# Two-layer hybrid decoder trunk: the MLP's up projection written in the down projection's form, with up and down units in one ordered stream

## The chip, the cores and the metric

The kernel runs on one core of one Trainium2 chip. The core has five engines with queues of their own: TensorE (PE) multiplies matrices and turns tiles, VectorE (DVE) and ScalarE (ACT) do elementwise work, GpSimd (POOL) does a little of it, and SyncE (SP) issues the DMAs. The metric is the device time of one execution in microseconds; lower is better. The kernel before takes 2218.81 us (median of three runs, 2218.77 to 2218.85).

## The reference

There are two layers over 256 tokens of width 2048, all in float32. A layer has a token-mixing part (gated linear attention beside stick-breaking attention, between one input and one output projection) and an MLP with 8192 hidden columns. The change is in the MLP:

```python
    mixed = jnp.concatenate([o_gla, o_sb], axis=-1)
    x = x + jnp.einsum('bse,ed->bsd', mixed, w_o)

    hm = rms_norm(x, mlp_norm)
    up = jnp.square(jax.nn.relu(jnp.einsum('bsd,df->bsf', hm, w_up)))
    return x + jnp.einsum('bsf,fd->bsd', up, w_down)
```

`w_up` is 2048 x 8192 and `w_down` 8192 x 2048, so each holds 64 MB per layer, and each layer multiplies 256 rows by both.

## The kernel before, in words

**Precision.** TensorE is fed with float32r, and each float32 operand is cut into a high part (a copy to float32r by ACT, L359 and L991) and a low part (the difference, by DVE, L361 and L992). A product of two operands is three matmuls: high by high, high by low, low by high.

**Residual and operands.** The residual stream lies in four tiles `xb[0..3]` of 128 partitions x 2 token blocks x 512 columns. `norm_operand` (L287) turns a tile on PE with the identity, four 128x128 turns to a bank, and writes the high and low parts of the turned, gain-scaled columns into operand tiles, a "pair" of two 128-row blocks each. The row factor of the norm isn't in the operand; it is applied later to the product.

**Up projection.** `mlp_up(q, g)` (L924) makes two times 256 hidden columns of quarter q. `unit_t` (L412) keeps the weights stationary and streams the activations: for each of the 16 row blocks and each of two 128-column halves one matmul of 512 columns (weight high by activations high and low side by side, L425) and one of 256 (weight low by activations high, L429). The result comes out with hidden columns on the partitions, which is what the down projection needs. `join` (L436) adds the two halves; then come the ReLU with the norm's row factor (L931, `row` laid along the free axis by `row_of`, L330), the square (L935), and `up_forms` (L942), which cuts the result into high and low (L939, L940). The scheduler orders this stage.

**Down projection.** `mlp_down(q)` (L962) adds quarter q's 2048 hidden rows into x in two units of 1024 output columns (`n2`). A unit runs over eight pairs j of row blocks. The activation block is now stationary and the weights stream, 512 columns to a matmul. An ordinary pair needs eight block products (two row blocks, two token blocks, two column halves) and has two steps of 12 matmuls. The pairs in `fast` (j = 1, 3, 5) use seven products of sums of blocks (a Winograd form of Strassen's scheme): `first` (L1038) makes three sums of the weights on DVE, `up_forms` has made three 128x128 sums of the activations before, and the pair has four steps of 6, 3, 6 and 6 matmuls. A unit so has 22 steps (0 to 21) and 5 x 24 + 3 x 21 = 183 matmuls, into eight PSUM banks m1 to m8. `drain` (after step 17), `drain_left` (after 20) and `drain_right` (after 21) add the banks into `xb`, one copy on ACT and 8 + 2 + 2 adds on DVE.

**Order.** PE, DVE and ACT take the down stage in an order written out by hand. Each step is prepared (sums, then `parts`: the high part on ACT, the low part on DVE) and appended to a queue; when four are in it (`LEAD`, L1099), the oldest one's matmuls are issued. So step k's matmuls stand behind the preparation of step k + 3, and what follows step k (a drain) stands on DVE and ACT in front of the preparation of step k + 4. The high and low tiles are a ring of four (L989, L990): step k + 4 is prepared into the tiles of step k, once its matmuls are through. Weights come in 1 MB loads on SP's queue, four pairs ahead. Each engine takes its instructions in this order, so one that waits holds back all behind it.

Of the kernel before, what the change touches and what calls it, by code (L numbers as in the profile page):

```python
# [16 lines left out]
P = 128  # L17
# [22 lines left out]
def trunk_kernel(  # L40
# [60 lines left out]
    ATT = ("v4", "lr", "lrT", "ha", "hh", "hl", "hA", "on", "dec", "S", "kdz")  # L101
    MLP = ("sx", "ts", "t4", "raw2")
# [9 lines left out]
    def down_psum():  # L112
        open_scope("psum", m=1)

# [155 lines left out]
    class Operand:  # L270


        def __init__(self):
            self.t = {}

# [11 lines left out]
    def norm_operand(op, n, key, l):  # L287

        for h2 in range(2):
            d = op.pair(2 * n + h2)  # L290
            pt = ps_tile()
            for j in range(2):
                for tt in range(NT):
                    c = (2 * h2 + j) * P
                    nc.tensor.transpose(  # L295
                        pt[:, j * T + tt * P : j * T + (tt + 1) * P],
                        xb[n][:, tt, c : c + P], ident,
                    )
            for j in range(2):
# [305 lines left out]
    for l in range(DEPTH):  # L605
# [296 lines left out]
        def residual(op, n, key, ll, ssq, acc, done):  # L902
            nc.vector.tensor_tensor(xb[n], acc, xb[n], ALU.add)
            after(1, lambda: norm_operand(op, n, key, ll))
            after(2, lambda: norm_squares(n, ssq))
            if n == 3:
                after(2, done)

# [3 lines left out]
        def mlp_stats():  # L912
            r = norm_finish(ssq)
            after(1, lambda: nxt.update(row=row_of(r)))

        for n in range(4):
            uo = unit(mixed, w_o[l], 0, n * 512, 512, (2, 3, 0, 1))
            residual(hm, n, "mlp", l, ssq, uo, mlp_stats)


        open_scope("sbuf", mlp=1)
        up = {}

        def mlp_up(q, g):  # L924
            if g == 0:
                up[q] = Operand()
                up[q].x = {}
            for b in range(2):
                i = 2 * g + b
# [8 lines left out]
        def split(d, t):  # L938
            nc.scalar.activation(d[:, :, 0, :], t, AF.Copy)  # L939
            nc.vector.tensor_tensor(d[:, :, 1, :], t, f32(d[:, :, 0, :]), ALU.subtract)  # L940

        def up_forms(op, i, t):  # L942


            if fast(i):
                a11, a21, a12, a22 = (t[:, k, r * P : (r + 1) * P] for k in range(2) for r in range(2))
                e = tmp("t2", [P, 3, P], bufs=4)
                d = op.x[i] = tmp("sx", [P, 3, 2, P], F32R, bufs=3)
                nc.vector.tensor_tensor(e[:, 2, :], a21, a11, ALU.subtract)
                nc.vector.tensor_tensor(a21, a21, a22, ALU.subtract)  # L950
                nc.vector.tensor_tensor(e[:, 0, :], a11, a21, ALU.subtract)
                nc.vector.tensor_tensor(e[:, 1, :], a12, e[:, 0, :], ALU.subtract)
                split(d, e)
            split(op.pair(i), t)

        def fast(i):
            return i in (1, 3, 5)

        hT = Operand()
        ssq2 = new_ssq()  # L960

        def mlp_down(q):  # L962


            op = up[q]
            end = q == 3 and l + 1 == DEPTH
            pairs = [(n2, j) for n2 in range(2) for j in range(8)]
            raws, banks = {}, {}
            begun = set()

            def load(x):
                if x >= len(pairs):
                    return
                n2, j = pairs[x]
                if x % 5 < 2:
                    r = tmp("raw2", [P, 2, 1024], bufs=2)
                else:
                    r = wpool.tile([P, 2, 1024], F32, tag="raw", name=nm("raw"))
                raws[x] = r
                r0 = (q * KT + 2 * j) * P  # L980
                nc.sync.dma_start(
                    r,
                    w_down[l][r0 : r0 + 2 * P, n2 * 1024 : (n2 + 1) * 1024].rearrange(
                        "(k p) n -> p k n", p=P
                    ),
                )

            def parts(r, n=2):
                hi = ppool.tile([P, 2, 512], F32R, tag="whi", name=nm("whi"), bufs=4)  # L989
                lo = ppool.tile([P, 2, 512], F32R, tag="wlo", name=nm("wlo"), bufs=4)  # L990
                nc.scalar.activation(hi[:, :n], r, AF.Copy)  # L991
                nc.vector.tensor_tensor(lo[:, :n], r, f32(hi[:, :n]), ALU.subtract)  # L992
                return hi, lo

            def mm(m, a, w, c, last):

                (ah, al), (wh, wl) = a, w
                o = banks[m]
                nc.tensor.matmul(o, ah, wh[:, c], start=m not in begun, stop=False)
                begun.add(m)  # L1000
                nc.tensor.matmul(o, ah, wl[:, c], start=False, stop=False)
                nc.tensor.matmul(o, al, wh[:, c], start=False, stop=last)

            def add(dst, a, b, sub=False):
                nc.vector.tensor_tensor(dst, a, b, ALU.subtract if sub else ALU.add)  # L1005

            def new_banks():
                begun.clear()
                for m in (5, 1, 6, 7, 2, 4, 3, 8):
                    banks[m] = pools["m"].tile([P, 512], F32, tag=f"m{m}", name=nm(f"m{m}_"))  # L1010

            def steps(x):

                n2, j = pairs[x]
                last = j == 7
                r = raws[x]
                d = op.t[j]
                x11, x21, x12, x22 = (xb[2 * n2 + c][:, tt, :] for c in range(2) for tt in range(2))

                def blk(k, tt):  # L1020
                    sl = slice(tt * P, (tt + 1) * P)
                    return d[:, k, 0, sl], d[:, k, 1, sl]

                def ext(i):
                    return op.x[j][:, i, 0, :], op.x[j][:, i, 1, :]

                def store(c, tt):
                    if end:
                        n = 2 * n2 + c
                        nc.sync.dma_start(  # L1030
                            ov[:, tt, n * 512 : (n + 1) * 512], xb[n][:, tt, :]
                        )

                if fast(j):
                    sums = {}
                    lastf = j == 5

                    def first():  # L1038
                        t13 = sums["t13"] = tmp("ts", [P, 2, 512], bufs=2)
                        t4 = sums["t4"] = tmp("t4", [P, 512], bufs=1)  # L1040
                        b12 = r[:, 0, 512:]
                        ends = r.rearrange("p k (c n) -> p (k c) n", c=2)[:, ::3, :]
                        nc.vector.tensor_tensor(  # L1043
                            t13, ends, b12.unsqueeze(1).to_broadcast([P, 2, 512]), ALU.add
                        )
                        add(b12, t13[:, 0, :], r[:, 1, 512:])
                        add(t4, b12, r[:, 1, :512])
                        return parts(r[:, 1, :].rearrange("p (c n) -> p c n", c=2))

                    def drain():  # L1050
                        dw = tmp("t2", [P, 512], bufs=4)
                        nc.scalar.activation(dw, banks[1], AF.Copy)
                        add(x12, banks[5], x12)
                        add(x22, banks[5], x22)
                        add(x11, banks[1], x11)
                        add(dw, banks[6], dw, True)
                        add(x12, dw, x12)
                        add(dw, banks[7], dw)
                        add(x21, x21, dw, True)
                        add(x22, dw, x22)  # L1060

                    return (
# [113 lines left out]
```

## Time and profile before

| what | time or share |
|---|---|
| median of three runs | 2218.81 us |
| the profiled execution, whole | 2219.26 us |
| its span (first to last instruction) | 2217.5 us |
| PE busy in it | 2208.2 us |
| DVE busy in it | 1627.6 us |
| ACT busy in it | 1170.7 us |
| DVE, wait for high parts by ACT at L359 | 417.7 us in 381 waits |
| ACT, wait for PE to free a high tile of the up stage (L425) | 338.1 us in 250 waits |

Busy times count each matmul with a modelled end that overlaps the next one, so PE's cost per instruction is read from the distance between starts, and not from the durations. Times in the rows of a timeline are microseconds from the start of the span. In a row, `x3` counts merged instructions, the first number is the start and the second the length, and what stands in square brackets is idle time of that engine ahead of it and what ended it. PEclk is the clock granted to TensorE, with 1.00 for full speed.

### The profile page before, as it was taken

How to read it: one execution, taken by the hardware profiler on the slowest of the kernel's cores; microseconds unless marked ns; L12 is line 12 of the kernel's file. 1: busy time of each engine (PE TensorE's matmuls, PEld its weight loads, DVE VectorE, ACT ScalarE, POOL GpSimd, SP SyncE). 2: the span in 40 equal slices, each digit the busy share in tenths (PEclk: the TensorE clock that was granted, in tenths of full speed). 3: DMA queues.
4: the chain of work that ended last, by engine and by line, in shares of the span. 5: the costliest groups of instructions: out<-in, count | busy, mean ns of one | idle time of the engine just before them, and what ended most of it. 6: DMA issues, size and time to landing. Idle time of an engine off the chain costs nothing.

```text
span 2217.5 us, 28469 instructions
## 1 busy us (share of the span) xinstructions
PE 2208.2 (100%) x11292; PEld 1857.2 (84%) x11292; DVE 1627.6 (73%) x2024; ACT 1170.7 (53%) x1499; POOL 39.1 (2%) x68
## 2 busy tenths in 40 slices
PE   9999999999999999999999999999999999999999
PEld 7988778888888888888888887788888888888887
DVE  5777556568868868967967775656697688688688
ACT  5555355555555455455556553545555555554553
POOL 0020000000000000000000200000000000000000
PEclk9999999999999999999999999999999999999999
DMA  6645446665664665665446544465656656656654
GB/s 225 196 153 168 139 149 229 189 190 190 209 189 172 222 184 179 206 198 188 172 136 197 171 158 142 150 233 184 190 183 216 190 189 208 185 177 217 186 178 141
DMA packets 250858, 409.05 MB, mean 184 GB/s; under 512 B 6651, under 2 KB 162883, under 8 KB 250725
## 3 DMA queue, kind: packets, MB, share of 16 engines
q1 hardware_dynamic: 250724, 407.24, 56.3%
q8 instruction: 88, 1.44, 0.3%
q14 instruction: 46, 0.37, 0.0%
HBM read 405.12 MB, written 2.10 MB: 184 GB/s over the span
## 4 chain that ended last, share of the span: by engine, by line
PE 98%; DVE 1%; issue 0%; DMA 0%; ACT 0%; POOL 0%; SPq 0%; POOLq 0%
PE acc L425 24%; PE acc L429 12%; PE acc L378 9%; PE acc L379 9%; PE acc L380 9%; PE ps L295 1%; PE ps L848 1%; PE ps L860 1%; PE ps L807 0%; PE ps L541 0%; PE ps L487 0%; DVE wlo L361 0%; PE ps L576 0%; PE ps L505 0%; DMA raw<-in_w_in_dram 0%
## 5 line engine op out<-in xcount | busy, mean ns | idle before, releaser
L361 DVE TENSOR_TENSOR wlo<-raw,whi 128x1024 fp32r<-128x1024 f32 (+2 forms) x530 | 630.3, 1193 | 418.7 <-ACT whi L359 417.7
L359 ACT ACTIVATE whi<-raw 128x1024 fp32r<-128x1024 f32 (+2 forms) x530 | 545.1, 1032 | 642.2 <-PE acc L425 338.1
L425 PE MATMUL acc<-act,whi 128*128 128x512 f32 x2304 | 813.2, 398 | 0.0
L429 PE MATMUL acc<-act,wlo 128*128 128x256 f32 x2304 | 645.1, 280 | 0.0
L425 PEld LDWEIGHTS acc<-act,whi 128*128 128x128 f32 x2304 | 432.9, 188 | 105.1
L429 PEld LDWEIGHTS acc<-act,wlo 128*128 128x128 f32 x2304 | 434.7, 189 | 0.4
L378 PE MATMUL acc<-whi,act 128*128 128x512 f32 (+2 forms) x960 | 368.1, 383 | 1.2 <-ACT act L303 0.9
L379 PE MATMUL acc<-wlo,act 128*128 128x512 f32 (+2 forms) x960 | 362.0, 377 | 0.4 <-DVE wlo L361 0.4
L380 PE MATMUL acc<-whi,act 128*128 128x512 f32 (+2 forms) x960 | 361.7, 377 | 0.0
L992 DVE TENSOR_TENSOR wlo<-raw,whi 128x1024 fp32r<-128x1024 f32 x256 | 305.6, 1221 | 48.2 <-ACT whi L991 44.6
L991 ACT ACTIVATE whi<-raw 128x1024 fp32r<-128x1024 f32 x256 | 266.4, 1059 | 122.9 <-PE acc L425 28.7
L378 PEld LDWEIGHTS acc<-whi,act 128*128 128x128 f32 x960 | 180.7, 188 | 36.5 <-issue 4.1
L380 PEld LDWEIGHTS acc<-whi,act 128*128 128x128 f32 x960 | 180.5, 188 | 33.9 <-issue 0.7
L379 PEld LDWEIGHTS acc<-wlo,act 128*128 128x128 f32 x960 | 180.7, 188 | 32.0 <-DVE wlo L361 1.2
L991 ACT ACTIVATE whi<-t 128x512 fp32r<-128x512 f32 x48 | 30.4, 633 | 157.1 <-DVE t L1005 45.1
L992 DVE TENSOR_TENSOR wlo<-ts,whi 128x1024 fp32r<-128x1024 f32 x48 | 58.8, 1225 | 2.3 <-ACT whi L991 2.3
L1043 DVE TENSOR_TENSOR ts<-raw 128x1024 f32<-128x1024 f32 x48 | 58.4, 1217 | 0.0
L940 DVE TENSOR_TENSOR act<-t,act 128x512 fp32r<-128x512 f32 x64 | 44.1, 689 | 10.9 <-ACT act L939 10.9
L991 ACT ACTIVATE whi<-ts 128x1024 fp32r<-128x1024 f32 x48 | 50.2, 1046 | 0.0
L440 DVE TENSOR_TENSOR t<-acc,t 128x512 f32<-128x512 f32 x72 | 49.2, 683 | 0.0
L935 ACT ACTIVATE t<-t 128x512 f32<-128x512 f32 x64 | 39.5, 617 | 12.8 <-DVE t L931 12.8
L931 DVE SCALAR_TENSOR_TENSOR t<-t,row 128x512 f32<-128x512 f32 x64 | 44.3, 692 | 2.2
(1160 smaller groups left out, 2760.0 us busy)
## 6 DMA issues: line engine op xcount, KB each, us to landing
raw<-in_w_down_dram SPq DMA_DIRECT2D x128, 1024.0 KB, 5.3
raw<-in_w_up_dram SPq DMA_DIRECT2D x128, 1024.0 KB, 5.8
raw<-in_w_in_dram SPq DMA_DIRECT2D x84, 1024.0 KB, 5.1
raw<-in_w_o_dram SPq DMA_DIRECT2D x32, 1024.0 KB, 5.0
raw<-in_w_in_dram SPq DMA_DIRECT2D x14, 512.0 KB, 6.6
raw<-in_w_in_dram SPq DMA_DIRECT2D x8, 544.0 KB, 3.8
out_dram<-xb SPq DMA_DIRECT2D x8, 256.0 KB, 2.2
xb<-in_x_dram SPq DMA_DIRECT2D x3, 512.0 KB, 7.6
```

Source lines behind the costliest of these rows:

```text
L359: newest["hi"] = nc.scalar.activation(h, r, AF.Copy).ins
L361: newest["lo"] = nc.vector.tensor_tensor(lo[:, q : q + step, :width], r, f32(h), ALU.subtract).ins
L378: nc.tensor.matmul(o, xh[:, sl], whi[:, j, :width], start=first, stop=False)
L379: nc.tensor.matmul(o, xh[:, sl], wlo[:, j, :width], start=False, stop=False)
L380: st["mm"] = nc.tensor.matmul(o, xl[:, sl], whi[:, j, :width], start=False, stop=last).ins
L425: nc.tensor.matmul(acc[:, f, :], whi[:, j, sl], op.both(k), start=(k == 0), stop=False, skip_group_check=True,)
L429: nc.tensor.matmul(acc[:, f, T:], wlo[:, j, sl], xh, start=False, stop=(k == KT - 1), skip_group_check=True,)
L440: nc.vector.tensor_tensor(t, acc[:, :, :T], t, ALU.add)
L931: nc.vector.scalar_tensor_tensor(t, t, 0.0, nxt["row"].unsqueeze(1).to_broadcast([P, 2, T]), ALU.max, ALU.mult,)
L991: nc.scalar.activation(hi[:, :n], r, AF.Copy)
L992: nc.vector.tensor_tensor(lo[:, :n], r, f32(hi[:, :n]), ALU.subtract)
L1043: nc.vector.tensor_tensor(t13, ends, b12.unsqueeze(1).to_broadcast([P, 2, 512]), ALU.add)
```

## The change

The up projection leaves `unit_t` and takes the form of the down projection: activation pairs of `hm` stationary, weights streaming, 1024 hidden columns to a unit, the same eight pairs with three of them by seven products, the same banks. `norm_operand` makes the sums of the activations for the three pairs (`sums=True`, `forms`). An up unit ends with tokens on the partitions, so its result has to be turned: `up_tail` combines the banks into two float32 tiles (one ACT copy and 4 + 2 + 2 adds on DVE) and applies the ReLU with the row factor on ACT, `turn` turns a tile on PE (eight 128x128 turns into two banks) and squares it out of PSUM on ACT, and `operand` cuts the pairs into high and low. For each up unit u this is done inside unit u + 1: `turn` stands behind steps 0 and 1 of it, `operand` behind steps 3, 4, 9 and 10.

All 16 units of a layer (two up and two down for each quarter) are now steps of one ordered stream with one queue; no stage is left to the scheduler, and the switch of PSUM pools between up and down is gone. The last part of the output projection's residual (n = 3), its `norm_operand` and the norm's statistics move into the first up unit. Gone are `mlp_up`, `join` for the up stage, `row_of` for the MLP, and the drains of the up stage.

In the order of the changed program, the instructions behind step 0 to step 10 of a unit that follows an up unit are, on ACT: high 3, two squares (turn 0), high 4, two squares (turn 1), high 5, high 6, cut of operand 0, high 7, two cuts of operand 1, high 8 to 12, cut of operand 2, high 13, cuts of operand 3, high 14. On DVE they are: the last two adds of the up unit, sums of pair 1 and low 2, low 3 to 6, cut of operand 0, low 7, four 128x128 sums and two cuts of operand 1, the sums of pair 3 and low 8, and so on.

```diff
@@ norm_operand @@
+    def fast(i):
+        return i in (1, 3, 5)
+
+    def split(d, t):
+        nc.scalar.activation(d[:, :, 0, :], t, AF.Copy)
+        nc.vector.tensor_tensor(d[:, :, 1, :], t, f32(d[:, :, 0, :]), ALU.subtract)
+
+    def forms(op, i, t, tag):
...
+            nc.vector.tensor_tensor(e[:, 2, :], a21, a11, ALU.subtract)
+            nc.vector.tensor_tensor(a21, a21, a22, ALU.subtract)
+            nc.vector.tensor_tensor(e[:, 0, :], a11, a21, ALU.subtract)
+            nc.vector.tensor_tensor(e[:, 1, :], a12, e[:, 0, :], ALU.subtract)
+            split(d, e)
+        split(op.pair(i), t)
+
-    def norm_operand(op, n, key, l):
+    def norm_operand(op, n, key, l, sums=False, banks=None):
...
+            if sums and fast(2 * n + h2):
...
+                forms(op, 2 * n + h2, t, "sxh")
+                continue
@@ the MLP @@
-        def mlp_up(q, g):
...
-                t = join(unit_t(hm, w_up[l], q * 2048 + i * 256))
-                nc.vector.scalar_tensor_tensor(
-                    t, t, 0.0, nxt["row"].unsqueeze(1).to_broadcast([P, 2, T]),
-                    ALU.max, ALU.mult,
-                )
-                nc.scalar.activation(t, t, AF.Square)
-                up_forms(up[q], i, t)
...
+        units = [(q, down, n2) for q in range(4) for down in range(2) for n2 in range(2)]
...
+        def up_tail(u):
...
+            def relu(h):
+                for tt in range(NT):
+                    nc.scalar.activation(
+                        y[h][:, tt, :], y[h][:, tt, :], AF.Relu, scale=rs["r"][:, tt : tt + 1]
+                    )
+
+            def sums():
...
+                nc.scalar.activation(y11, banks[1], AF.Copy)
+                add(dw, banks[6], y11, True)
+                add(y12, banks[5], dw)
+                add(y21, banks[7], dw)
+                add(y22, banks[5], y21)
+
+            def left():
+                add(y[0][:, 0, :], banks[2], y[0][:, 0, :])
+                add(y[0][:, 1, :], banks[4], y[0][:, 1, :], True)
+                relu(0)
+
+            def right():
+                add(y[1][:, 0, :], banks[3], y[1][:, 0, :])
+                add(y[1][:, 1, :], banks[8], y[1][:, 1, :])
+                relu(1)
...
+        def turn(u, h):
...
+            for i in range(2):
+                pt = bank(((5, 7), (1, 6))[h][i])
+                for j in range(2):
+                    for tt in range(NT):
+                        c = (2 * i + j) * P
+                        nc.tensor.transpose(
+                            pt[:, j * T + tt * P : j * T + (tt + 1) * P],
+                            y[h][:, tt, c : c + P], ident,
+                        )
+                nc.scalar.activation(t[:, i].rearrange("p j t -> p (j t)"), pt, AF.Square)
+
+        def operand(u, i):
...
+            forms(op, 4 * n2 + i, ys[u]["t", i // 2][:, i % 2], "sx")
...
+        def begin(u):
+
+            if u == 0:
+                def stats():
+                    norm_squares(3, ssq)
+                    rs["r"] = norm_finish(ssq)
+
+                return {
+                    0: lambda: norm_operand(hm, 3, "mlp", l, sums=True, banks=(5, 7)),
+                    4: stats,
+                }
+            if units[u - 1][1]:
+                return {}
+            p = u - 1
+            return {
+                0: lambda: turn(p, 0), 1: lambda: turn(p, 1),
+                3: lambda: operand(p, 0), 4: lambda: operand(p, 1),
+                9: lambda: operand(p, 2), 10: lambda: operand(p, 3),
+            }
...
+        def emit():
+            u, k, products, w = queue.pop(0)
...
+            products(w)
+            (sums, left, right), extra = tails[u]
+            if k in extra:
+                extra[k]()
+
+            for at, fn in ((17, sums), (20, left), (21, right)):
+                if k == at:
+                    fn()
...
+            for x in range(8 * len(units)):
+                load(x + 4)
...
+                for i, (prepare, products) in enumerate(steps(x)):
+                    if j == 1 and i == 0:
+
+                        while queue[0][0] < u:
+                            emit()
+                    queue.append((u, count, products, prepare()))
+                    count += 1
+                    if x == 1 and i == 0:
+                        residual(3, uo)
+                    if len(queue) >= LEAD and (u or count >= LEAD):
+                        emit()
```

More of the change, by code (lines that the diff above doesn't have):

```diff
@@ L899, in trunk_kernel, with residual @@
                 after(3 + hp, lambda e=2 * g + hp, t=gate, c=hp * 2 * P: gated(e, t, c))
[L902 to L907, printed above, removed]
         hm = Operand()
         ssq = new_ssq()
-        def mlp_stats():
-            r = norm_finish(ssq)
-            after(1, lambda: nxt.update(row=row_of(r)))
+        def residual(n, acc):
+            nc.vector.tensor_tensor(xb[n], acc, xb[n], ALU.add)
@@ new lines, in mm, with add @@
+        def mm(m, a, w, c, last):
+            (ah, al), (wh, wl) = a, w
+            if m not in begun:
+                banks[m] = bank(m)
+            o = banks[m]
+            nc.tensor.matmul(o, ah, wh[:, c], start=m not in begun, stop=False)
+            begun.add(m)
+            nc.tensor.matmul(o, ah, wl[:, c], start=False, stop=False)
+            nc.tensor.matmul(o, al, wh[:, c], start=False, stop=last)
+        def add(dst, a, b, sub=False):
+            nc.vector.tensor_tensor(dst, a, b, ALU.subtract if sub else ALU.add)
@@ L1121, in mlp_down @@
             while queue:
[L1122 to L1123 removed]
+                emit()
+            if l + 1 < DEPTH:
                 for n in range(4):
```

312 lines of the change are left out of this document (146 added, 166 removed).

## The prediction

> **What bounds the kernel now.** I read the page first: the busy shares and the chain that ended last.
>
> ```profile
> span 2217.5 us, 28469 instructions
> PE 2208.2 (100%) x11292; PEld 1857.2 (84%) x11292; DVE 1627.6 (73%) x2024; ACT 1170.7 (53%) x1499; POOL 39.1 (2%) x68
> PE 98%; DVE 1%; issue 0%; DMA 0%; ACT 0%; POOL 0%; SPq 0%; POOLq 0%
> ```
>
> PE is the bound nearly everywhere, and 73% of DVE is an average. So the windows come next: the first up quarter, and its two down units.
>
> ```profile
> 420.00:507.00 87.00, 86.93 (x507) 75.97 (x506) 59.84 (x80) 47.41 (x63) 0.59 (x2) 1.00 0.61 186
> 507.60:549.00 41.40, 41.40 (x185) 34.27 (x184) 36.62 (x41) 23.54 (x26) 0.00 (x0) 1.00 0.50 176
> 549.00:590.50 41.50, 41.50 (x185) 34.39 (x184) 38.99 (x45) 21.72 (x23) 0.00 (x0) 1.00 0.62 203
> ```
>
> Columns: length, then busy PE, weight loads, DVE, ACT, POOL; granted clock, DMA share, GB/s. DVE is at 69% in the up stage and at 94% (38.99 of 41.50) in the second down unit. The change gives the up stage the form in which DVE is nearly full, and adds DVE work. Whether DVE keeps up decides.
>
> **The change on PE.** The starts of the units' first matmuls, and of a few more:
>
> ```profile
> 417.49 0.39 PE L425 MATMUL acc<-act,whi 128*128 128x512 f32 x1
> L999 PE MATMUL m__793_4423<-whi,act x13: 389/389/395, 507.7 to 544.4; 128*128 128x512 f32 x13
> L999 PE MATMUL m__860_4747<-whi,act x13: 389/389/389, 549.2 to 585.9; 128*128 128x512 f32 x13
> L999 PE MATMUL m__1040_5854<-whi,act x13: 389/389/395, 681.1 to 717.8; 128*128 128x512 f32 x13
> 1110.77 0.39 PE L1002 MATMUL m__1604_9043<-whi,act 128*128 128x512 f32 x1
> ...
> 507.66 0.40 PE L999 MATMUL m__793_4423<-whi,act 128*128 128x512 f32 x1
> 513.11 0.39 PE L999 MATMUL m__793_4423<-whi,act 128*128 128x512 f32 x1
> 517.87 0.39 PE L999 MATMUL m__793_4423<-whi,act 128*128 128x512 f32 x1
> 420.47 0.87 PE ps L295 x8
> ...
> L295 PE MATMUL ps<-ident,xb 128*128 128x128 f32 x128 | 17.8, 283 | 1.4 <-DVE xb L1005 1.1 <-DMA xb<-in_x_dram 0.3
> ```
>
> An ordinary pair takes 513.11 - 507.66 = 5.45 for 24 matmuls, a pair by seven products 4.76 for 21: 0.227 a matmul, 183 x 0.227 = 41.5 a unit, which is 549.2 - 507.7. A quarter takes 681.1 - 507.7 = 173.4, so its up stage takes 173.4 - 2 x 41.5 = 90.4. The layer's MLP runs from 417.49 to 1111.0, or 693.5.
>
> After, two up units cost 2 x 41.5 on PE and 32 turns. The row of the chain of waits has eight turns in 0.87, so a unit's 16 cost 1.74. A quarter's PE work is 4 x 41.5 + 2 x 1.74 = 169.5, a gain of 3.9, or 31 over the eight quarters. If nothing else waited, that would be all.
>
> Here a page stands against the trace: the Trainium skill ("TensorE: Matmul & The Clock Gate", Part 4: PE-mode transpose) gives about 275 ns for a turn in a kernel's context. By it a unit's turns would cost 16 x 0.275 = 4.4 instead of 1.74, and the PE gain would be a loss of 1.4 a quarter; the trace's 109 ns decides.
>
> **The change on DVE and ACT: what is late.** I walk through the unit that follows an up unit (the second up unit and the first down unit of each quarter). Prices are distances between starts; the order is that of the changed program. Rows of the second down unit, which has the same steps (PE began it at 549.2):
>
> ```profile
> 549.36 0.68 DVE L1005 TENSOR_TENSOR xb<-m__795_4425,xb 128x512 f32<-128x512 f32 x1
> 549.96 0.68 DVE L1005 TENSOR_TENSOR xb<-m__796_4426,xb 128x512 f32<-128x512 f32 x1
> 550.55 1.21 DVE L1043 TENSOR_TENSOR ts<-raw 128x1024 f32<-128x1024 f32 x1
> ...
> 553.14 1.22 DVE L992 TENSOR_TENSOR wlo<-raw,whi 128x1024 fp32r<-128x1024 f32 x1
> 554.27 0.68 DVE L992 TENSOR_TENSOR wlo<-t,whi 128x512 fp32r<-128x512 f32 x1
> ...
> 556.09 3.52 DVE L992 TENSOR_TENSOR wlo<-raw,whi 128x1024 fp32r<-128x1024 f32 x3
> 559.52 1.22 DVE L1043 TENSOR_TENSOR ts<-raw 128x1024 f32<-128x1024 f32 x1
> ...
> 562.12 1.22 DVE L992 TENSOR_TENSOR wlo<-raw,whi 128x1024 fp32r<-128x1024 f32 x1
> ```
>
> An add is 0.60, the three sums 553.14 - 550.55 = 2.59, a low part 3.43 / 3 = 1.14, a half-size one 0.68. Step 8 (the first of pair 3) is due on PE at 549.2 + 5.45 + 4.76 + 5.45 = 564.9, and its low part is there at 562.12 + 1.22 = 563.3: a margin of 1.5. What the change puts in front of it has these prices:
>
> ```profile
> 618.38 0.29 DVE L949 TENSOR_TENSOR t<-t 128x128 f32<-128x128 f32 x1
> 618.70 0.29 DVE L950 TENSOR_TENSOR t<-t 128x128 f32<-128x128 f32 x1
> 621.26 0.55 DVE L940 TENSOR_TENSOR sx<-t,sx 128x384 fp32r<-128x384 f32 x1
> 621.73 0.68 DVE L940 TENSOR_TENSOR act<-t,act 128x512 fp32r<-128x512 f32 x1
> ```
>
> ```profile
> 553.33 0.63 ACT L991 ACTIVATE whi<-t 128x512 fp32r<-128x512 f32 x1 [5.63 <-DVE t L1005]
> 553.87 1.04 ACT L991 ACTIVATE whi<-ts 128x1024 fp32r<-128x1024 f32 x1
> 554.85 1.06 ACT L991 ACTIVATE whi<-raw 128x1024 fp32r<-128x1024 f32 x1
> 565.05 1.06 ACT L991 ACTIVATE whi<-raw 128x1024 fp32r<-128x1024 f32 x1 [1.15 <-PE m__863_4750 L1002]
> 602.97 0.58 ACT L439 ACTIVATE t<-acc 128x512 f32<-128x512 f32 x1
> 619.99 0.51 ACT L939 ACTIVATE sx<-t 128x384 fp32r<-128x384 f32 x1
> ```
>
> A small sum is 0.32, a cut 0.48 (384 columns) or 0.61 (512) on DVE, 0.46 or 0.55 on ACT; a high part 1.0; a square or ReLU, which the trace has not on these tiles, I price as the copy out of PSUM at 602.97, 0.55 (between 0.46 and 0.63 by the neighbours: 0.3 less or more over four). The row at 565.05 waits for step 7, whose matmuls end by the cadence at 564.85: a result is there 0.2 to 0.25 later.
>
> Now the clock of one unit, with 0 where its first matmul starts. *PE* wants step 2 at 5.45 + 1.74 = 7.2, steps 4 and 5 at 9.2 and 10.6, step 8 at 7.2 + 4.76 + 5.45 = 17.4 (its low part one matmul later, 17.6). *DVE* ends the up unit's last add at 0.85 (0.25 and 0.60), the sums at 3.4, low 2 at 4.6, low 3 at 5.25. *ACT* can do high 3 only from 3.5, the first two squares to 5.2, high 4 to 6.2; so low 4 ends at 7.4 after an idle 1.0. Then ACT stands in the squares of the second turn, which PE ends at 7.2: squares to 8.0, high 5 to 9.1. Low 5 so ends at 10.3, after 1.75 idle, just in time. From here DVE never rests: low 6 to 11.4, operand 0 to 12.0, low 7 to 13.2, four small sums to 14.5, 0.6 for ACT, two cuts to 16.2, sums of pair 3 to 18.8, low 8 to 20.0. **PE stands 20.0 - 17.6 = 2.4.** The 1.5 of margin and the 1.74 of turns don't cover operands 0 and 1 (0.6 + 3.0) and 2.8 of waiting for ACT.
>
> In the second up unit the same comes again. DVE: low 9 to 12 to 24.1, operand 2 to 24.7, low 13 to 25.8, operand 3 (a pair by seven products again) to 28.9, sums to 31.5, low 14 to 32.6. PE is there at 19.75 + 4.76 + 5.45 = 30.0, low part 30.2: another 2.4. In the first down unit operand 3 is an ordinary pair (0.6 instead of 3.1) and step 14 is on time. I take 2.4 + 2.4 + 2.4 and 0.1 for the second down unit, whose first bank is drained at the last moment: 7.3 a quarter. Bounds: without any waiting for ACT (3.4 before step 8, 4.0 before step 14) 0.9 is left, 4.9 less 4.0. Upwards, the second down unit of the trace has low 2 at 554.36 for a need at 554.65, so 0.3 to spare: if the units without operands stood 2.4 once too, it would be 12.1.
>
> **The entry of a layer.** `norm_operand` of n = 3 and the statistics now stand in the first up unit's order: eight turns (0.87, which the old 693.5 has as well), then four copies and four differences that take turns, and two squares with their small chain ahead of high 8. The rows around it suggest 0.8 at step 8, where 1.5 of margin is left; bounds 0 and 3. Costed at nothing: the loads (four pairs ahead, same bytes), the sums for n < 3 (in the output projection, where DVE has room), the gone `row_of`, the up tail's adds and ReLUs (behind step 21 they end at 1.5 on ACT, before high 2).
>
> **Sum.** Before, a layer's MLP takes 693.5. After: 4 x (169.5 + 7.3) + 0.87 + 0.8 = 708.9, which is 15.4 more; 31 for two layers. Span 2217.5 + 31 = 2248.5. The profiled execution took 2219.26, 0.45 above the median, so I take the median plus 31: **2250 us**.
>
> **Rivals.** *DVE keeps up (faster).* If ACT's waits don't add up, 0.9 a quarter is left: 31 - 8 x 0.9 - 3 = 21 gained, 2198. The sign turns at 3.9 - (0.87 + 0.8) / 4 = 3.5 of standing a quarter. For it: DVE's work fits. A down unit has 39.0 (the window), an up unit some 2.6 less (four adds), operands add 6.0 to the second up unit and 4.2 to the first down unit: 36.4 + 42.4 + 43.2 + 39.0 = 161 of 169.5. Against: the ring of four tiles lets DVE run only three steps ahead, so the average doesn't help where operands bunch. 8%. *Half of it:* only step 8 stands, 1.5 to 2 each time: 3 to 4 a quarter, no change. 3%. *The lateness spreads* to all four units, 12.1 a quarter: 2250 + 8 x 4.8 = 2288. The 0.3 above speaks for it, the shorter up drain (8 adds instead of 12) against it. 5%. *PE slows after each stand.* If the 21 matmuls after each of 24 stands ran at half speed, 24 x 4.76 = 114 would be added: 2364. The only gap at hand is this one:
>
> ```profile
> 1112.68 1.53 PE L295 MATMUL ps<-ident,xb 128*128 128x128 f32 x12 [1.09 <-DVE xb L1005]
> ```
>
> ```profile
> 1112.00:1114.00 2.00, 1.32 (x13) 1.32 (x13) 2.00 (x5) 2.00 (x5) 0.00 (x0) 1.00 0.40 59
> ```
>
> The clock stayed at 1.00 over 1.09 of idling; a gap of 2.4 isn't in the trace. The Trainium skill ("TensorE: Matmul & The Clock Gate", What's actually happening) has the clock fall only after a whole idle window of about 3.4 us, which would leave these gaps alone. 2%. *Turns that don't overlap:* at the mean length of 283 ns that the groups give a turn (they overlap in the trace: eight in 0.87), PE would work 2 x 16 x 0.17 = 5.6 more a quarter; it would fill some of the standing, so at most 2250 + 45 = 2295. 2%.
>
> **How the numbers follow.** The forecast has 80%, and its own range is 2238 to 2264 (1.5 more or less a quarter). Slower by over 0.2% (4.4 us, about what a measurement of this kernel can tell from no change) is 80 + 5 + 2 + 2 = 89%, no change 3%, faster 8%. For 8 in 10 I widen it to 2229 and 2275, two thirds of the way to the point where the sign turns (2219) and to 2288, since the unknown prices lie between these bounds.
>
> **What would show it.** In the changed profile, PE should stand about 2.4 behind "DVE wlo" at the first matmuls of pair 3 in 16 units and of pair 5 in 8, the granted clock at 1.00; the up units should have 183 matmuls at 0.227, and 16 turns in 1.74. DVE should wait near 1 and 1.8 for ACT's high parts of steps 4 and 5, ACT for PE's second turn. If PE has no idle time in these units, the walk is wrong; if it has, but at other steps, its order is.

## The result, and the profile after

The changed kernel takes 2269.67 us (median of 4 runs, 2266.16 to 2270.38); the kernel before takes 2218.82 beside it. The ratio is 1.0226, with a 95% interval of 1.0208 to 1.0244: slower by 50.9 us. The span went from 2217.5 to 2268.6, or 51.1.

The page of the changed kernel: its span, busy time by engine, and the chain of work that ended last, by engine.

```profile
span 2268.6 us, 27081 instructions
PE 2213.3 (98%) x10376; PEld 1822.8 (80%) x10376; DVE 1825.4 (80%) x2286; ACT 1250.8 (55%) x1623; POOL 38.0 (2%) x64
PE 85%; DVE 11%; ACT 3%; issue 1%; DMA 0%; SPq 0%; POOL 0%; ACTq 0%
```

PE has 916 matmuls fewer than before and is busy for longer. DVE and ACT now hold 14% of the chain, where they had 1%: work of PE was traded for waits, and some of the matmuls that remain became slower.

The starts of the first units of layer 1, and then the windows from unit to unit (length; busy PE, weight loads, DVE, ACT, POOL; granted clock, DMA share, GB/s). In order the windows hold the second up unit, the two down units, and the two up units of the next quarter.

```profile
L995 PE MATMUL m__672_3632<-whi,act x13: 388/389/468, 419.9 to 458.0; 128*128 128x512 f32 x13
L995 PE MATMUL m__753_3995<-whi,act x13: 388/389/477, 462.7 to 506.3; 128*128 128x512 f32 x13
L995 PE MATMUL m__836_4375<-whi,act x13: 388/389/476, 511.0 to 553.6; 128*128 128x512 f32 x13
```

```profile
462.70:511.00 48.30, 45.48 (x200) 36.97 (x200) 42.41 (x53) 28.94 (x38) 0.00 (x0) 0.96 0.50 173
511.00:558.30 47.30, 45.21 (x200) 37.10 (x200) 42.28 (x51) 27.87 (x35) 0.00 (x0) 0.96 0.46 159
558.30:599.80 41.50, 41.50 (x184) 34.34 (x184) 39.05 (x44) 21.75 (x23) 0.00 (x0) 1.00 0.57 204
599.80:641.30 41.50, 41.50 (x184) 34.38 (x184) 37.67 (x41) 22.40 (x25) 0.00 (x0) 1.00 0.62 224
641.30:690.90 49.60, 45.54 (x200) 36.99 (x200) 42.58 (x53) 29.06 (x38) 0.00 (x0) 0.97 0.49 170
```

Two kinds of unit stand side by side. A unit that follows a down unit runs at the pace of PE, 41.5 us, in the up projection too: the new form is as cheap on PE as it should be. A unit that follows an up unit takes 47.3 to 49.6 in these windows, and its granted clock is below 1. (Over both layers such a unit takes 45.7 to 49.6; in the one of 45.7, which began at 869.7, the clock stayed at 1.00.)

The place where that time goes, on PE, in the first down unit (began at 511.0). A row is start, duration, line, output and inputs; in brackets stand the idle time before it and what ended it.

```profile
528.50 0.39 PE L995 MATMUL m__836_4375<-whi,act 128*128 128x512 f32 x1
530.98 0.78 PE L997 MATMUL m__836_4375<-wlo,act 128*128 128x512 f32 x1 [2.09 <-DVE wlo L986]
531.55 0.63 PE L998 MATMUL m__836_4375<-whi,act 128*128 128x512 f32 x1
531.98 0.63 PE L995 MATMUL m__843_4406<-whi,sx 128*128 128x512 f32 x1
```

The first matmul of step 8 runs, and the second waits for the low part: from 528.50 to 530.98 is 2.48 instead of 0.23, so PE stands for 2.25. Then it goes on at 531.98 - 531.55 = 0.43 a matmul instead of 0.23 (the distance between two starts is called the pitch below). The windows around it show for how long (the clock is the third value from the right); the last one lies within the slow stretch:

```profile
526.00:529.00 3.00, 2.89 (x13) 2.06 (x11) 2.97 (x4) 1.42 (x2) 0.00 (x0) 1.00 0.85 311
529.00:533.00 4.00, 2.02 (x5) 1.64 (x6) 3.97 (x6) 2.53 (x3) 0.00 (x0) 0.75 0.00 0
533.00:536.00 3.00, 3.00 (x12) 2.39 (x11) 2.29 (x3) 2.50 (x4) 0.00 (x0) 0.76 0.37 68
536.00:540.00 4.00, 4.00 (x20) 3.30 (x19) 3.97 (x5) 1.50 (x3) 0.00 (x0) 1.00 0.86 284
531.10:534.40 3.30, 3.30 (x8) 2.62 (x9) 2.77 (x3) 2.23 (x3) 0.00 (x0) 0.50 0.00 0
```

The matmuls have the long pitch from 530.98 until shortly after 534.11; from 534.50 on it is 0.23 again. That is some 3.4 us at half the clock (0.50), which costs another 3.4 x (1 - 0.227 / 0.427) = 1.6 us.

Why the low part is late can be read from DVE in the same unit:

```profile
517.23 1.23 DVE L986 TENSOR_TENSOR wlo<-ts,whi 128x1024 fp32r<-128x1024 f32 x1 [0.96 <-ACT whi L985]
520.11 2.36 DVE L986 TENSOR_TENSOR wlo<-raw,whi 128x1024 fp32r<-128x1024 f32 x2 [1.66 <-ACT whi L985]
522.39 0.68 DVE L296 TENSOR_TENSOR act<-act,act 128x512 fp32r<-128x512 f32 x1
...
525.99 0.56 DVE L296 TENSOR_TENSOR sx<-t,sx 128x384 fp32r<-128x384 f32 x1 [0.59 <-ACT sx L295]
526.51 0.69 DVE L296 TENSOR_TENSOR act<-act,act 128x512 fp32r<-128x512 f32 x1
527.12 1.22 DVE L1118 TENSOR_TENSOR ts<-raw 128x1024 f32<-128x1024 f32 x1
...
529.71 1.22 DVE L986 TENSOR_TENSOR wlo<-raw,whi 128x1024 fp32r<-128x1024 f32 x1
```

DVE waits 0.96 and 1.66 for ACT's high parts of steps 4 and 5, then cuts two operands and makes the sums of pair 3, and ends low part 8 at 530.93: 19.9 after the unit began. ACT in turn waited for the second turn of PE:

```profile
518.05 0.60 ACT L1086 ACTIVATE act<-m__846_4421 128x512 f32<-128x512 f32 x1 [0.86 <-PE m__846_4421 L1082]
```

In the second up units a second stand follows at step 14, the first of pair 5. Two of these units, the first and the second quarter's, both stands of each:

```profile
482.65 0.50 PE L997 MATMUL m__753_3995<-wlo,act 128*128 128x512 f32 x1 [2.08 <-DVE wlo L986]
...
495.50 0.50 PE L997 MATMUL m__753_3995<-wlo,act 128*128 128x512 f32 x1 [0.74 <-DVE wlo L986]
...
661.27 0.50 PE L997 MATMUL m__1051_5395<-wlo,act 128*128 128x512 f32 x1 [2.07 <-DVE wlo L986]
...
673.79 0.50 PE L997 MATMUL m__1051_5395<-wlo,act 128*128 128x512 f32 x1 [1.99 <-DVE wlo L986]
```

In the first of them the clock fell after step 8. Those slow matmuls gave DVE time, and the stand at step 14 shrank to 0.74 idle. In the second the clock did not fall, and the second stand is as long as the first. Over both layers five of the eight second stands are short and three are long.

Last, the entry of the layer on PE: the last matmul of the output projection, and the first of the up projection.

```profile
417.57 0.39 PE L414 MATMUL acc<-whi,act 128*128 128x512 f32 x1
419.88 0.47 PE L995 MATMUL m__672_3632<-whi,act 128*128 128x512 f32 x1 [1.92 <-DVE xb L940]
```

Pitch 2.31 instead of 0.23: the first matmul wants a bank of PSUM out of which the residual add (L940) still reads the output projection's last accumulator.

Summed over all stands of the trace, in both layers together:

| term | predicted us | measured us |
|---|---|---|
| PE work: matmuls and turns | -29.3 | -29.6 |
| stand at step 8, in 16 units | 16 x 2.4 = 38.4 | 16 x 2.24 = 35.9 |
| stand at step 14, in 8 units | 8 x 2.4 = 19.2 | 11.0 |
| stand in the second down unit | 0.8 | 0 |
| entry of a layer, twice | 1.6 | 4.9 |
| matmuls slowed after a stand | 0 | 15 x 1.6 = 24.0 |
| not assigned | | 4.8 |
| sum | 30.7 | 51.0 |

Of the 4.8, 2.6 are the first matmul after each of the 24 stands, which has a pitch of 0.34 instead of 0.23 also where the clock doesn't fall. Of the entry's 4.9, 2 x 2.08 are the gap shown above. So one term that the forecast set to zero, the clock, is larger than the whole difference between forecast and result.

### The profile page after: what moved, and what is told of

Its sections match the earlier page's. It is cut to its first block, busy times and chain, and to the rows that moved or that the text cites. A ratio compares the mean times of both kernels' runs of the same rounds, so it can differ in the third digit from the quotient of the medians.

```text
span 2268.6 us, 27081 instructions
## 1 busy us (share of the span) xinstructions
PE 2213.3 (98%) x10376; PEld 1822.8 (80%) x10376; DVE 1825.4 (80%) x2286; ACT 1250.8 (55%) x1623; POOL 38.0 (2%) x64
## 4 chain that ended last, share of the span: by engine, by line
PE 85%; DVE 11%; ACT 3%; issue 1%; DMA 0%; SPq 0%; POOL 0%; ACTq 0%
PE acc L412 9%; PE acc L413 9%; PE acc L414 9%; DVE wlo L986 4%; PE acc L459 3%; PE acc L463 1%; DVE act L296 1%; DVE ts L1118 1%; ACT whi L985 1%; DVE raw L1001 1%; DVE t L1001 1%; ACT act L1086 1%; DVE sx L296 1%; ACT sx L295 1%; PE ps L882 1%
## 5 line engine op out<-in xcount | busy, mean ns | idle before, releaser
L986 DVE TENSOR_TENSOR wlo<-raw,whi 128x1024 fp32r<-128x1024 f32 x512 | 610.1, 1221 | 82.4 <-ACT whi L985 79.3
L985 ACT ACTIVATE whi<-raw 128x1024 fp32r<-128x1024 f32 x512 | 532.8, 1056 | 198.4 <-PE acc L414 10.0
L395 DVE TENSOR_TENSOR wlo<-raw,whi 128x1024 fp32r<-128x1024 f32 (+2 forms) x274 | 317.5, 1165 | 194.9 <-ACT whi L393 193.7
L393 ACT ACTIVATE whi<-raw 128x1024 fp32r<-128x1024 f32 (+2 forms) x274 | 273.5, 1004 | 290.9 <-PE acc L414 243.1
L1118 DVE TENSOR_TENSOR ts<-raw 128x1024 f32<-128x1024 f32 x96 | 117.0, 1219 | 0.0
L459 PE MATMUL acc<-act,whi 128*128 128x512 f32 x256 | 91.9, 402 | 0.0
L463 PE MATMUL acc<-act,wlo 128*128 128x256 f32 x256 | 71.8, 280 | 0.0
L1001 DVE TENSOR_TENSOR raw<-ts,raw 128x512 f32<-128x512 f32 x96 | 66.4, 692 | 3.3
L1001 DVE TENSOR_TENSOR t<-raw 128x512 f32<-128x512 f32 x96 | 66.4, 692 | 3.3
L986 DVE TENSOR_TENSOR wlo<-t,whi 128x512 fp32r<-128x512 f32 x96 | 65.7, 684 | 0.0
L459 PEld LDWEIGHTS acc<-act,whi 128*128 128x128 f32 x256 | 48.1, 188 | 11.1
```

What stands on the lines that cost most here:

```text
L393: newest["hi"] = nc.scalar.activation(h, r, AF.Copy).ins
L395: newest["lo"] = nc.vector.tensor_tensor(lo[:, q : q + step, :width], r, f32(h), ALU.subtract).ins
L459: nc.tensor.matmul(acc[:, f, :], whi[:, j, sl], op.both(k), start=(k == 0), stop=False, skip_group_check=True,)
L463: nc.tensor.matmul(acc[:, f, T:], wlo[:, j, sl], xh, start=False, stop=(k == KT - 1), skip_group_check=True,)
L1118: nc.vector.tensor_tensor(t13, ends, b12.unsqueeze(1).to_broadcast([P, 2, 512]), ALU.add)
```

## The experiments

The theory after this reading: DVE's work ahead of step 8 makes PE stand, the stand itself lowers the clock for some 3.4 us, and the entry has a bank conflict of its own. The rival to its second part was that the slow matmuls have another cause (the load of the unit, say) and would stay if PE never idled. The kernels' line numbers differ by a few from the changed kernel's.

**Filling the stands with matmuls.** 18 matmuls on a tile of zeros, into an accumulator that they leave as it is, are put ahead of the steps at which PE stands (the tile is filled once, at the start of the kernel):

```
+            if u and not units[u - 1][1] and (k == 8 or k == 14 and not units[u][1]):
+                for _ in range(18):
+                    nc.tensor.matmul(banks[2][:, :256], tri, zero, start=False, stop=False)
```

> Eighteen products of zeros (256 columns, near 0.12 us each, 2.1 us together) stand on PE ahead of step 8 in each unit that follows an up unit, and ahead of step 14 in the second up units; they add zero to bank m2. Theory (VectorE is late by some 2.2 us at these steps, and the idling then lowers TensorE's clock for about 3.4 us): the fillers take the place of the standing, the granted clock stays at 1.00, the 25 us of slowed matmuls go, and the second stand of five units, which the slow clock had shortened to 0.9, is 2.2 again: about 2251 us. Rival (the clock falls for another reason, such as the load of the unit): the slowed matmuls stay, 2268 to 2275 us.

Measured: 2253.03 (2252.55 to 2254.63), granted clock 1.00. PE at step 8 of the second up unit:

```profile
479.10 2.31 PE L1184 MATMUL m__754_3999<-zero,tri 128*128 128x256 f32 x18
481.24 0.40 PE L999 MATMUL m__754_3999<-whi,act 128*128 128x512 f32 x1
```

With 432 matmuls more, the kernel is 16.6 us faster. The low part comes as late as ever, but PE doesn't idle while it waits, and no slow matmul is left behind a stand of these steps. By the table this should bring 24.0, less some 1.3 for each of the five short second stands, which grow back: 24.0 - 6.5 = 17.5. The spans of the two profiled executions differ by 2268.6 - 2250.8 = 17.8. The stands cause the slow clock.

**Shorter gaps.** The same edit with 8 and with 4 matmuls instead of 18 shortens each gap without removing it, and so asks from what length on it costs clock.

> The same with eight fillers, near 1 us: PE then stands about 1.2 us instead of 2.2. If a gap of 1.2 us is too short to lower the clock, the time is that of eighteen fillers, about 2251 us; if a gap of any length lowers it, about 2269 us.

> Four fillers of zeros: PE then stands near 1.7 us at the 24 places. If the clock falls by the length of one gap and the bound lies between 1.3 and 1.7 us, slowed matmuls are back in most of them, 2265 to 2270 us; if it lies above, 2253 us as with eight and eighteen fillers.

Measured: 2253.72 (2253.64 to 2255.0) with 8, 2253.82 (2253.76 to 2254.96) with 4. The clock is 1.00, or 0.999 in the profiled execution with 4: there it fell once, behind the gap at the entry of layer 1, and behind no stand of step 8 or 14. The gaps at step 8 of the second up unit, first with 8, then with 4:

```profile
480.31 1.11 PE L1184 MATMUL m__754_3999<-zero,tri 128*128 128x256 f32 x8
...
482.76 0.50 PE L1001 MATMUL m__754_3999<-wlo,act 128*128 128x512 f32 x1 [1.11 <-DVE wlo L990]
```

```profile
481.57 0.63 PE L1184 MATMUL m__754_3999<-zero,tri 128*128 128x256 f32 x4
482.04 0.39 PE L999 MATMUL m__754_3999<-whi,act 128*128 128x512 f32 x1
484.01 0.50 PE L1001 MATMUL m__754_3999<-wlo,act 128*128 128x512 f32 x1 [1.58 <-DVE wlo L990]
```

Stands of 484.01 - 482.04 - 0.23 = 1.74 us (1.58 idle) occur 24 times in that kernel, and after none does the clock fall. At 2.24 (some 2.08 idle) it fell in 12 of 16 at step 8. Four small matmuls, half a microsecond, take the whole loss of clock at these stands away.

**The operands at other steps.**

```
-                3: lambda: operand(p, 0), 4: lambda: operand(p, 1),
-                9: lambda: operand(p, 2), 10: lambda: operand(p, 3),
+                6: lambda: operand(p, 0), 7: lambda: operand(p, 1),
+                12: lambda: operand(p, 2), 13: lambda: operand(p, 3),
```

> The cuts of the four operands stand behind steps 6, 7, 12 and 13 instead of 3, 4, 9 and 10. Theory (VectorE has too much work within three steps' reach, wherever the operands stand): the standing comes at later steps and stays near 5 and 2.6 us in the two units of a quarter, 2262 to 2278 us. Rival (only the place ahead of the sums of pair 3 is bad): the standing and the slow clock go, about 2200 us.

Measured: 2264.87 (2264.37 to 2266.04), clock 0.989. PE at step 11 (the last of pair 3) of the second up unit, and the window behind it:

```profile
484.86 0.50 PE L995 MATMUL m__779_4095<-whi,act 128*128 128x512 f32 x1 [0.86 <-ACT whi L985]
486.12 0.50 PE L997 MATMUL m__779_4095<-wlo,act 128*128 128x512 f32 x1 [0.76 <-DVE wlo L986]
```

```profile
486.00:490.00 4.00, 3.88 (x11) 3.07 (x12) 3.97 (x5) 1.66 (x2) 0.00 (x0) 0.66 0.68 222
```

The stands go from steps 8 and 14 to steps 11 and 17 and remain about as long together. So the place is not the cause; what is left is the amount of work ahead of the bunched steps, which the runs with eight products below put to the test. Here two gaps of 0.86 and 0.76 idle lie 1.26 apart, each shorter than the 1.11 and 1.58 that did nothing alone, and the clock falls behind them (0.66 in the window); it does in 12 of the 16 units with such a pair at step 11 (seven of eight in layer 1, five of eight in layer 2). What decides is worked out in the last section.

**The entry's bank.** The first up unit takes banks 5 and 7 before 2 and 4, so that those of its turns, not those of step 0, fall on the output projection's last accumulators:

```
+                if u == 0:
+                    pre.extend((bank(5), bank(7)))
...
-                    0: lambda: norm_operand(hm, 3, "mlp", l, sums=True, banks=(5, 7)),
+                    0: lambda: norm_operand(hm, 3, "mlp", l, sums=True, banks=pre),
```

> In the first up unit of a layer the banks m5 and m7 are allocated ahead of m2 and m4, so that the turns of the last residual tile, and not step 0, lie on the banks of the output projection's last product. Theory (step 0 waits 2.2 us for the residual add that reads these banks): 2.2 us less in each of two layers, about 2265 us. Rival (the turns behind step 0 then wait as long): no change, 2269 to 2270 us.

Measured: 2265.8 (2262.19 to 2267.97), 3.9 less than the changed kernel in its own runs. The two ranges overlap, and the clock fell 13 times in the profiled execution, not 15, so the trace says more than the time. The entry on PE:

```profile
417.72 0.39 PE L414 MATMUL acc<-whi,act 128*128 128x512 f32 x1
417.95 0.39 PE L995 MATMUL m__674_3634<-whi,act 128*128 128x512 f32 x1
```

The pitch at the entry is 0.23; the 2.08 us are gone in each layer.

**Less work on DVE, by giving it to GpSimd.** The operands' cuts (high and low parts) and small sums go to GpSimd, which has 98% of its time free; `forms` and `split` take the engine as an argument:

```
-            forms(op, 4 * n2 + i, ys[u]["t", i // 2][:, i % 2], "sx")
+            forms(op, 4 * n2 + i, ys[u]["t", i // 2][:, i % 2], "sx", nc.gpsimd)
```

> The whole cut of the operands (sums, high and low parts) is done by GpSimd, which is idle in this stage; VectorE and ScalarE keep the rest in the same order. Theory (VectorE's amount of work makes the standing): some 4 to 6 us less on VectorE per unit, no standing, clock 1.00; less 47 us of standing and 25 of slowed matmuls: 2195 to 2205 us. Rival (ScalarE's wait for the second turn makes it): steps 4 and 5 stay late and some 1 to 2 us of standing a unit remain, about 2240. Second rival: VectorE's instructions get longer while GpSimd runs, by the 1.75 us that an operation of 512 columns takes there, and nothing is gained: over 2260.

Measured: 2285.93 (2285.6 to 2287.08), 16 us slower than the changed kernel, where 2195 to 2205 had been expected; it is the second rival that came. The costliest groups, first of the changed kernel, then of this one:

```profile
L986 DVE TENSOR_TENSOR wlo<-raw,whi 128x1024 fp32r<-128x1024 f32 x512 | 610.1, 1221 | 82.4 <-ACT whi L985 79.3
L1118 DVE TENSOR_TENSOR ts<-raw 128x1024 f32<-128x1024 f32 x96 | 117.0, 1219 | 0.0
```

```profile
L989 DVE TENSOR_TENSOR wlo<-raw,whi 128x1024 fp32r<-128x1024 f32 x512 | 643.7, 1292 | 73.3 <-ACT whi L988 69.7
L1121 DVE TENSOR_TENSOR ts<-raw 128x1024 f32<-128x1024 f32 x96 | 142.8, 1488 | 0.0
L299 POOL TENSOR_TENSOR act<-act,act 128x512 fp32r<-128x512 f32 x64 | 139.9, 2200 | 0.0
```

The instructions that stayed on DVE became longer: the low parts by 71 ns on average (512 of them: 36 us), the sums by 269 (96: 26 us). These means mix two kinds. The 422 low parts that ran while GpSimd was idle took 1219 ns, as before, and the 88 that ran beside it for over half of their time 1645 (two lie between); of the sums 72 took 1215 and 24, all beside GpSimd, 2308. By the two pages the busy time of DVE rose from 1825.4 to 1863.4 though 184 instructions had left it. The Trainium skill ("GPSIMD Engine Reference", Specifications) says that GpSimd shares its SBUF interfaces with VectorE and contends with DVE instructions that have two inputs in SBUF; both groups are such, and the runs agree. So this kernel says nothing against the theory of DVE's load, which it had not lightened; the forecast for it was wrong.

**Less work on DVE, by eight products for pair 3.** In the 16 units that follow an up unit, pair 3 is computed the ordinary way:

```
+        def few(u):
+            return bool(u) and not units[u - 1][1]
...
-            if fast(j):
+            if fast(j) and not (j == 3 and few(u)):
```

This kernel uses the operand's blocks as they lie, and one of them has been overwritten by a difference: pair 3 of those units is computed from that in its place. The unit then has 20 steps, and its drains move up by two.

> In the units that follow an up unit, pair 3 is done by eight products: three matmuls more on PE (0.68 us in each of 16 units, 11 us in all), and on VectorE no weight sums and two low parts instead of four: 4.2 us less in such a unit. Theory (VectorE's amount of work): no standing and no slow clock, 2270 - 47 - 25 + 11 = about 2208 us. Rival (ScalarE's wait for the turns): standing at step 8 stays by 1 us or more, 2235 us or above.

Measured: 2211.2 (2209.75 to 2213.04), clock 0.999; the ratio to the kernel before is 0.9967 (0.9955 to 0.9978). The second up unit:

```profile
463.53:507.59 44.06, 44.06 (x203) 36.49 (x202) 38.06 (x48) 27.27 (x36) 0.00 (x0) 1.00 0.54 189
```

PE is busy in all of it. Three matmuls more (0.7 us) and five instructions less on DVE (48 instead of 53, busy for 38.06 instead of 42.41) take away the unit's stands and its slow matmuls together: 44.1 instead of 48.3. The clock of 0.999 comes from one slow stretch at 1519.1, behind the entry of layer 2.

**The squares one step later.** With this, ACT's high part of step 4 no longer stands behind them:

```
-                0: lambda: turn(p, 0), 1: lambda: turn(p, 1),
+                0: lambda: turn(p, 0), 1: lambda: (square(p, 0), turn(p, 1)), 2: lambda: square(p, 1),
```

> The squares of each turn stand one step later on ScalarE, behind the next high part, so that the high parts of steps 4 and 5 no longer wait for the turns. Theory (VectorE's amount of work, the waits for ScalarE are a small part): 0.45 us less standing in each of 16 units, 7 us, and the slow clock mostly stays, about 2262 us. Rival (the 2.7 us of waits for ScalarE make the standing): it goes at step 8, about 2215 to 2230 us.

Measured: 2261.56 (2260.47 to 2263.72). The stand at step 8 of the second up unit:

```profile
482.48 0.50 PE L997 MATMUL m__753_3995<-wlo,act 128*128 128x512 f32 x1 [1.79 <-DVE wlo L986]
```

1.79 idle instead of 2.08. ACT's waits are a small part of what is late; the walk had 2.8 of waiting for ACT ahead of step 8, and of these this order gives back 0.3. The shorter stand still lowers the clock, at step 8 in 11 of 16 units.

**Pair 3 by eight products, with its fourth block kept, and the entry's banks.** The difference goes into a tile of its own, so that the block itself remains; to make room, the weight sum `t4` takes its tile from another pool (`t2`). The edits of the entry are included.

```
-            nc.vector.tensor_tensor(a21, a21, a22, ALU.subtract)
-            nc.vector.tensor_tensor(e[:, 0, :], a11, a21, ALU.subtract)
+            nc.vector.tensor_tensor(s, a21, a22, ALU.subtract)
+            nc.vector.tensor_tensor(e[:, 0, :], a11, s, ALU.subtract)
...
+            if fast(j) and not (j == 3 and few(u)):
```

> Eight products for pair 3 in the units that follow an up unit, as in the run "two", and its operand now keeps the block that the sums overwrote, with the difference as a fourth block of its own (0.13 us more on VectorE for each such cut); the banks are allocated as in "entry". Theory (VectorE's amount of work made the standing, the bank of step 0 the entry): no standing, clock 1.00, 2211 - 4 = 2207 us, below the kernel before. Rival (the standing went in "two" because of its other data or order): some standing is back, 2215 us or more.

Measured: 2205.01 (2204.23 to 2205.57, 5 runs), beside 2219.03 for the kernel before: ratio 0.9937, interval 0.9925 to 0.995. Its page:

```profile
PE 2195.4 (100%) x10424; PEld 1815.9 (82%) x10424; DVE 1755.7 (80%) x2206; ACT 1225.9 (56%) x1591; POOL 38.0 (2%) x64
PE 99%; DVE 1%; DMA 0%; issue 0%; ACT 0%; SPq 0%; POOL 0%; ACTq 0%
```

PE is the bound again, in 99% of the chain. Faster than both kernels by 14 and 65 us.

## Why the prediction was right, and where it wasn't

The direction was right; the size was 20 us short (31 forecast, 51 measured). The time lies outside the forecast's own range of 2238 to 2264 (by its working, 1.5 in each of eight quarters, 2262) and inside the wide one, whose upper end was drawn towards another rival, the lateness that spreads. A term that the forecast had put at nothing brought it there, so it is in part luck that the wide range holds it. Step by step:

- **PE's work**: right, -29.3 against -29.6. The unit at 599.8 takes 41.5 in the new form, and a unit's first eight turns cost 514.81 - 513.94 = 0.87, as the chain of waits of the changed kernel has them below. The rival with turns that don't overlap falls. So, for this kernel, do the 275 ns of the Trainium skill ("TensorE: Matmul & The Clock Gate", Part 4: PE-mode transpose).

```profile
513.94 0.44 PE m__839_4390 L1082 x4
514.38 0.44 PE m__840_4396 L1082 x4
514.81 0.23 PE m__843_4406 L995
```

- **DVE's load in the four units**: 36.4, 42.4, 43.2 and 39.0 were worked out, in the order of the units; 37.67, about 42.5, 42.28 and 39.05 stand in the windows. The rival "DVE keeps up" had argued from this total, 161 of 169.5. The total does fit, and PE stands all the same, since operands 0 and 1 and the sums come together ahead of step 8. With pair 3 by eight products it keeps up.
- **The walk through the unit**: right in place and size. Low part 8 was to end at 20.0 and ends at 19.9; the two waits for ACT were to be 1.0 and 1.75, and are 0.96 and 1.66. The stand at step 8 is 2.24 where 2.4 was forecast, in all 16 units and no others, so the lateness did not spread.
- **The stand at step 14**: the place is right. The size, 2.4 in 8 units, holds in three of them (2.15 to 2.2). In the other five it is 0.74 to 1.02; in each of them the matmuls after step 8 had been slow, which let DVE catch up. It was forecast for an undisturbed clock.
- **The entry**: the term was mis-sized, 0.8 a layer for 2.45. Its cost was looked for at step 8, in ACT's and DVE's extra work, and lay for the most part (2.08) at step 0, in the bank that the old order had not needed so early. No step of the working asked which banks the first up unit takes. In the run with the banks in another order the 2.08 are gone in both layers.
- **The clock**: the step that failed. The rival "PE slows after each stand" had 2%, with two grounds: a gap of 1.09 in the trace had not lowered the clock, and the idle window of about 3.4 us of the Trainium skill ("TensorE: Matmul & The Clock Gate", What's actually happening) was longer than a stand. The first is true, and was stretched to gaps of twice that length; the second doesn't hold here, where 2.08 us of idling was enough. The rival's price was wrong the other way: 21 matmuls at half speed, 4.76, where only the matmuls of some 3.4 us are slow, 1.6. 15 falls x 1.6 are 24, where the rival had 114. An unknown reaction with bounds of 0 and 114 needed more than 2%, and a middle: half of the 24 stands, at the 1.6 that was measured only afterwards, would have put the forecast at 2269.

## What to carry to other kernels

When a change puts an engine's load near full, walk through one unit in order, with starts and waits: the average said that DVE fits, the walk found the stand to within 0.2 us. Price every new stand of PE of about 2 us with the slow matmuls behind it as well (1.6 here, after 15 of 19); if it can't be removed, a few cheap matmuls in the gap are worth more than they cost. And a cheaper form needn't be used everywhere: eight products where DVE is short and seven elsewhere took 2205, seven everywhere 2266 with the same banks.

## What was not expected of the hardware

- **Short gaps lower the clock.** Idle gaps of 2.0 to 2.1 us were followed by some 3.4 us at half the clock in 15 of 19 cases at steps 8 and 14 of the changed kernel, and gaps of 1.78 in 11 of 16 at step 8 with the squares one step later. Gaps of 1.54 to 1.61 did nothing in 24 of 24. Pairs of 0.86 and 0.76 did, with the operands at other steps. The gap of 1.92 at the entry did nothing in the changed kernel, but in other profiled executions the clock fell behind it: once each with four fillers, with pair 3 by eight products and with the squares later, and twice with the cuts on GpSimd. So it is not the length of one gap alone. The Trainium skill ("TensorE: Matmul & The Clock Gate", section "Why this matters for your kernels") advises against idle gaps of over about 3 us; here gaps of two thirds of that were enough.
- **What decides is the standing within fixed stretches of 3.413 us.** In the changed kernel the 15 slow stretches end at 486.68, 534.46, 677.83 and so on to 2200.18, and these times lie whole multiples of 3.4133 us apart, to within 0.02 us: 14, 56 and at last 502 of them. Cut the time at these marks and add up in each piece how long PE stands (pitch less 0.227). In the 15 pieces ahead of a slow one the sum is 2.15 to 2.25 us, and in all others 2.09 or less, also around the four stands of over 2.2 after which the clock stayed, since there a mark cuts the stand in two. Three other traces with many falls have marks at the same distance. Their sums ahead of a slow piece, and in all other pieces, are: 1.94 or more, and 1.92 or less, with the operands at other steps, where the two gaps fall into one piece; 1.89 or more, and 1.95 or less, with the squares later; 1.99 or more, and 2.09 or less, with the banks in another order. So about 1.9 to 2.1 us of standing in one piece was enough, and whether a stand of 2.24 lies within one piece is chance. This is read from the traces; no run set out to test it.
- **Work on GpSimd lengthens DVE's instructions**: 1215 to 2308 ns for the sums of 128x1024 that ran beside it, 1219 to 1645 for the low parts of that size. The means over the kernel, in which GpSimd was busy for 17% of the span, rose only to 1488 and 1292.
